# A mixture-of-experts decoder layer: experts of ranks 17 to 21 as blocks of 64 and 32 tokens on unsplit weights, a new order of blocks, twelve table tiles

## The chip, the cores and the metric

The kernel runs on one core of one Trainium2 chip. The metric is the device time of one execution in microseconds (us); lower is better. The input is one sequence of 2048 tokens with 1024 channels, in float32.

## The reference

One layer: a Conformer convolution mixer, then a mixture of 32 gated-MLP experts, each with a residual add, and a final RMSNorm. The change concerns the experts alone. In short:

```python
x = x + g1 * conformer_conv(h, ...)
h = rmsnorm(x, norm_ffn_g) * (1 + sc2) + sh2
# routing: the best of 4 groups, in it the best 2 of 8 experts, gate = p(group) * softmax(top 2)
for each expert e, for its tokens xb:
    hid = silu(xb @ w_gate[e]) * (xb @ w_up[e])      # 1024 -> 512
    y = hid @ w_down[e]                              # 512 -> 1024
    out[token] += gate * y
x = rmsnorm(x + g2 * out)
```

Each expert has 6.3 MB of weights (1024 x 512 twice and 512 x 1024, float32). The 4096 assignments (2048 tokens, two experts each) fall unevenly on the experts.

## The kernel before, in words

The first half of the run makes the convolution mixer and the routing, chunk by chunk; the change does not touch it. Its products on the expert side are a table per expert in DRAM (`tab_d`: token number, row to add to, gate), the normalized tokens (`x1n_d`) and the residual sum (`x2acc`), to which the experts' results are added by scatters.

*Ranks.* The experts are sorted by their number of tokens; rank p is a place in this sorting, and its expert number is read at run time (`number`, line 966, a load of `Ei` on SyncE, issued after the last weight load so far). `PROFILE` (line 48) says for each rank how many blocks of 128 tokens it has and how many tokens (32 or 64) one small block more takes. What a rank has beyond its profile goes through a loop at the end (`further_blocks`), which runs as often as there are such blocks.

*Two kinds of blocks.* A block of 128 tokens (b >= 0, "split") multiplies in three products: weights and tokens are each split into a high and a low part of type fp32r, and high x high, low x high and high x low are accumulated (`products`, lines 1068 to 1085). A small block (b < 0, "unsplit") multiplies the raw float32 weights once; with 64 tokens two column groups of the array work side by side, with 32 tokens four (m = 128 / tokens), each on its share of the contraction.

*Weights.* `load_expert` (line 990) loads an expert in six raw tiles of 1 MB (four of gate and up, two of down) from `RAWB` = 5 rotating buffers, all on SyncE's queue (line 998). If the rank has blocks of 128, ScalarE copies each raw half tile to its high part (line 1005) and VectorE subtracts (line 1006); the results fill `HLB` = 12 tiles, that is one expert. A raw tile is free when it is split and when the last unsplit matmul on it is done; a high or low tile when the last split block of its expert is done with it.

*Steps.* `ORDER` (line 64) lists all blocks as (rank, block), 50 of them; each becomes a `Step`. For step n the loop at the end of the kernel issues the gate and up matmuls, in their middle the transposes of step n-1's hidden values, then the activation, the gather of step n+2 (`ahead`), the load and token transposes of step n+1 (`start`), and the down matmuls and scatter of step n-1. A scheduler that orders each engine's instructions ahead of time may move them against this. `gather` (line 1020) loads the rank's tables when its first block comes (`load_table`, line 972): a tile `ft` for its blocks of 128 (line 979) and a tile `rt` for its small block (`small_rows`, line 724: 128 / tokens small loads and one VectorE instruction). Both have four buffers, and a table tile is in use until its block's scatter has landed. These loads stand in SyncE's queue among the weight loads. Gathers (line 1034) and scatters (line 1127) are issued by GpSimd.

*The end.* Rank 1 comes last. After its first block stand the overflow loop and the final normalization of all 2048 rows (`final_norm`), which reads what all other ranks have added; rank 1's own three blocks are normalized and written one by one (`norm`).

Of the kernel before, what the change touches and what calls it, by code (L numbers as in the profile page):

```python
# [13 lines left out]
I32 = mybir.dt.int32  # L14
# [7 lines left out]
P = 128  # L22
# [22 lines left out]

PROFILE = ([(3, 32), (3, 0), (2, 64), (2, 32), (2, 0), (1, 64), (1, 64)] + [(1, 32)] * 6 + [(1, 0)] * 9
           + [(0, 64)] * 8 + [(0, 32)] * 2)

EARLY = 2
EREST = PROFILE[0][1]
NEARLY = EARLY * 128 + EREST
# [4 lines left out]
LATE = 1  # L60
assert PROFILE[LATE][1] == 0


ORDER = [
# [5 lines left out]
]  # L70
RAWB, HLB = 5, 12
FIRSTL = 1
LASTU = 600

# [53 lines left out]
def moe_kernel(ctx, tc, x, xT, cols, ada, fing, w_in, w_out, b_r, wgu, wd, out):  # L128
    nc = tc.nc
# [15 lines left out]
    tabv = tab_d[:].rearrange("(e o b) c -> e o b c", o=P, b=NRB)  # L145
# [60 lines left out]
    def pool(name, bufs=1, stack=None, **kw):  # L206
        return (stack or p1).enter_context(tc.tile_pool(name=name, bufs=bufs, reuse_waits="tile", **kw))
# [484 lines left out]
    def first_rows():  # L692

        with urgent():
            pc = bank("acc", "pcs")
            nc.tensor.matmul(pc[:, :E], ones_bf[:], Cpre[:], start=True, stop=True)
            k = sm.tile([P, 2, E], F32, tag="fk", name="fk", bufs=1)
            V.tensor_tensor(k[:, 0], oh0[:], pc[:, :E], op=OP.mult)
            V.tensor_reduce(e0[:, 0:1], k[:, 0], axis=AX.X, op=OP.add)

            d = sm.tile([P, 1 + EARLY], F32, tag="fd", name="fd", bufs=1)
            for b in range((NEARLY + P - 1) // P):
                V.tensor_scalar(d[:, 1:2], pcol[:], e0[:, 0:1], float(b * P), op0=OP.add, op1=OP.add)
                V.tensor_scalar(d[:, 1:2], d[:, 1:2], float(NEARLY), None, op0=OP.is_lt)
                V.scalar_tensor_tensor(Cpre[:], oh0[:], d[:, 1:2], Cpre[:], op0=OP.mult, op1=OP.add)
            e = nc.sync.value_load(E0[0:1, 0:1], min_val=0, max_val=E - 1)
            ft = ep.tile([P, EARLY, 3], I32, name="fte")
            nc.sync.dma_start(ft[:], tabv[ds(e, 1), :, 0:EARLY, :].rearrange("e o b c -> (e o) b c"))
            rt = ep.tile([P, 3], I32, name="rte")
            small_rows(rt, e, EARLY, EREST)  # L710
            for b in range(-1, EARLY):
                m = P // EREST if b < 0 else 1
                t = rt if b < 0 else ft[:, b, :]
                xg = ep.tile([P, D // m], F32, name=f"xge{b + 1}")
                Q.indirect_dma_start(out=xg[:], out_offset=None, in_=x1n_d[:T0[-1], :].rearrange("t (m n) -> (t m) n", m=m),
                                     in_offset=bass.IndirectOffsetOnAxis(ap=t[:, 0:1].bitcast(U32), axis=0))
                early[b] = (t, xg)
            return e
# [2 lines left out]
    table_end = [None]  # L721
    sync = mybir.DependencyInfo(mybir.DependencyClass.Sync, mybir.DependencyReason.DATA)

    def small_rows(rt, e, b, rest):

        m = P // rest
        for g in range(m):
            nc.sync.dma_start(rt[g * rest:(g + 1) * rest, :], tabv[ds(e, 1), 0:rest, b, :].rearrange("e o c -> (e o) c"))
        V.tensor_scalar(rt[:, 0:2], rt[:, 0:2], float(m), pgrp[m][:], op0=OP.mult, op1=OP.add)

    wrv = col("w_r").rearrange("p (k n) -> p k n", k=KD)
# [69 lines left out]
    for s in range(NS + LAG_OUT):  # L801
        c, j = divmod(s, KD)
# [47 lines left out]
    for m in g2t:  # L850
        w, n = P // m, D // m
# [60 lines left out]
    nfull, cap, rest = (prof[:, q:q + 1] for q in range(3))  # L912
# [41 lines left out]
    xr = pool("xr", 1, p3)  # L954
# [8 lines left out]
    es, tix = {0: first}, {}  # L963
    loads, scattered = [], []

    def number(p):
        if p not in es:
            with tc.issue_after(loads[-1].ins):
                es[p] = nc.sync.value_load(Ei[0:1, p:p + 1], min_val=0, max_val=E - 1)
        return es[p]  # L970

    def load_table(p):

        nf, rest = PROFILE[p]
        ft = rt = None
        if nf:
            ft = xr.tile([P, 4, 3], I32, tag="ft", name="ft", bufs=4)
            if p:
                nc.sync.dma_start(ft[:, :nf, :], tabv[ds(number(p), 1), :, 0:nf, :].rearrange("e o b c -> (e o) b c"))
            else:  # L980
                for b in range(EARLY, nf):
                    for o, c, n in ((0, b, EREST), (P - EREST, b + 1, 0)):
                        nc.sync.dma_start(ft[o:o + (P - EREST if n else EREST), b, :],
                                          tabv[ds(number(p), 1), n:(P if n else EREST), c, :].rearrange("e o c -> (e o) c"))
        if p and rest:
            rt = xr.tile([P, 3], I32, tag="rt", name="rt", bufs=4)
            small_rows(rt, number(p), nf, rest)
        tix[p] = ft, rt

    def load_expert(p, tiles=range(6)):  # L990

# [2 lines left out]
        for n in tiles:  # L994
# [4 lines left out]
            raws.append((r,))  # L999
            if p is not None and PROFILE[p][0]:  # L1000
                h = hl[2 * n].tile([P, 2048], F32R, tag="hl", name="wh")
# [7 lines left out]
    class Step:  # L1009
# [10 lines left out]
        def gather(s):  # L1020
            if s.p == 0 and s.b in early:
                t, s.xg = early[s.b]
                s.entry(t)
                return
            if s.p not in tix:
                load_table(s.p)
            ft, rt = tix[s.p]
            t = ft[:, s.b, :] if s.split else rt
            s.entry(t)
            s.fetch()  # L1030

# [111 lines left out]

    steps = []
    for p, b in ORDER:
        steps.append(Step(p, b, 1 if b >= 0 else P // PROFILE[p][1]))
    ws = {}

    def start(s):
# [61 lines left out]
    for n in range(len(steps) + 1):  # L1211
        s = steps[n] if n < len(steps) else None
        t = steps[n - 1] if n > 0 else None
# [38 lines left out]
def host_layout(inputs):  # L1252
# [12 lines left out]
    prof = np.zeros((P, 3), np.float32)  # L1265
    for p, (n, r) in enumerate(PROFILE):
        prof[p] = (n, n * P + r, r)
# [40 lines left out]
```

## Time and profile before

| | us |
|---|---|
| median of 3 runs | 1640.28 |
| lowest and highest | 1636.06, 1649.84 |
| the profiled execution | 1638.36 |
| its span, first to last instruction | 1636.6 |

In the span TensorE is busy 1474.6 us (90%), VectorE 1116.2 (68%), ScalarE 977.9 (60%) and GpSimd 731.7 (45%). The expert stage begins near 828 us. An engine's busy time is the union of its instructions; an idle time is put down to what ended it. A matmul's end is modelled, so that neighbours overlap in the rows: the distance from one start to the next is what one costs. PE is TensorE, DVE VectorE, ACT ScalarE, POOL GpSimd, SPq SyncE's queue.

### The profile page before, as it was taken

The page shows a single profiled execution, that of the slowest core. Times are in us where ns is not written, and L with a number is a line of the kernel's source. Part 1 is how long each engine was busy: PE and PEld are TensorE (multiplying, and loading weights), DVE is VectorE, ACT ScalarE, POOL GpSimd, SP SyncE. Part 2 cuts the span into 40 slices and gives each one's busy share as a digit, 9 for nine tenths or more (in the row PEclk, how much of TensorE's full clock was granted, in tenths as well). Part 3 has the DMA queues.
Part 4 walks back from the last instruction along what each step waited for, and adds up shares of the span by engine and source line. Part 5 has one row for each costly group of instructions (what it writes and reads, how often), then busy time and mean ns, then how long its engine had stood idle before and what let it go on. Part 6 is the DMA issues. An engine that isn't in the chain of part 4 may idle for free. (4 is left out here: it accounts for less than half of the span.)

```text
span 1636.6 us, 24063 instructions
## 1 busy us (share of the span) xinstructions
PE 1474.6 (90%) x8269; PEld 1067.9 (65%) x8269; DVE 1116.2 (68%) x1777; ACT 977.9 (60%) x1602; POOL 731.7 (45%) x564
## 2 busy tenths in 40 slices
PE   6987997999889999987987899999999999898984
PEld 4765675677667777756854366556777767675663
DVE  2564988688988899885462257254588778786465
ACT  5576768766876788445440255234487668675553
POOL 0268699768778787854231122121122212122222
PEclk9988999899999999998999999999999999999997
DMA  8696796776766558594548999989899889887987
GB/s 323 234 367 240 245 297 211 254 257 241 254 242 214 184 193 289 189 309 147 220 140 230 370 343 355 344 292 376 310 383 346 306 276 383 284 339 213 367 309 268
DMA packets 123646, 455.98 MB, mean 279 GB/s; under 512 B 25594, under 2 KB 29058, under 8 KB 98946
## 3 DMA queue, kind: packets, MB, share of 16 engines
q1 hardware_dynamic: 93842, 362.48, 61.7%
q0 software_dynamic: 14224, 40.43, 9.8%
q10 hardware_dynamic: 15456, 51.51, 7.9%
q8 instruction: 66, 1.08, 0.3%
q14 instruction: 58, 0.48, 0.1%
HBM read 374.24 MB, written 80.13 MB: 278 GB/s over the span
## 5 line engine op out<-in xcount | busy, mean ns | idle before, releaser
L467 POOL TENSOR_TENSOR acc<-acc,prod 128x512 f32<-128x512 f32 x321 | 426.9, 1330 | 59.2 <-ACT prod L461 38.0
L473 DVE SCALAR_TENSOR_TENSOR acc<-u,colt,acc 128x512 f32<-128x512 f32 x497 | 371.3, 751 | 49.3 <-PE acc L444 39.5
L1006 DVE TENSOR_TENSOR wl<-wraw,wh 128x1024 fp32r<-128x1024 f32 x260 | 304.9, 1218 | 53.0 <-ACT wh L1005 51.6
L461 ACT ACTIVATE prod<-u,colt 128x512 f32<-128x512 f32 x385 | 268.8, 720 | 91.7 <-POOL acc L467 74.7
L1005 ACT ACTIVATE wh<-wraw 128x1024 fp32r<-128x1024 f32 x264 | 265.0, 1059 | 87.8 <-DMA wraw<-in_wgu 43.0
L1082 PE MATMUL pg<-wh,xh 128*128 128x512 f32 x464 | 150.5, 399 | 13.6 <-ACT wh L1005 7.5
L1082 PE MATMUL pg<-wl,xh 128*128 128x512 f32 x464 | 149.0, 396 | 0.9 <-DVE wl L1006 0.7
L1082 PE MATMUL pg<-wh,xl 128*128 128x512 f32 x464 | 149.0, 396 | 0.0
L1084 PE MATMUL pg<-wraw,xh 128*32 128x256 f32 (+1 forms) x992 | 121.9, 470 | 5.9 <-DMA wraw<-in_wgu 3.4
L1034 POOL DMA_INDIRECT xg<-x1n_d,ft x27 | 33.7, 1250 | 203.4 <-DMA rt<-tab_d 75.3
L1051 ACT ACTIVATE psx<-psx,modc,A 128x128 f32<-128x128 f32 x232 | 90.3, 441 | 52.0 <-PE psx L1046 37.1
L1127 POOL DMA_INDIRECT x2acc<-ys,ft x24 | 57.5, 2398 | 142.6 <-DVE ys L1124 119.0
L371 PE MATMUL pg<-hh,wh 128*128 128x512 f32 x256 | 106.6, 416 | 14.0 <-DMA wh<-wi_d 9.8
L1082 PEld LDWEIGHTS pg<-wh,xh 128*128 128x128 f32 x464 | 87.2, 190 | 38.0 <-ACT wh L1005 10.6
L371 PE MATMUL pa<-hh,wh 128*128 128x512 f32 x256 | 103.2, 403 | 7.1 <-DVE u L408 6.6
L1100 ACT ACTIVATE sg<-pg 128x256 f32<-128x256 f32 (+1 forms) x79 | 26.3, 370 | 135.5 <-PE pg L1082 66.9
L373 PE MATMUL pg<-hh,wl 128*128 128x512 f32 x256 | 104.7, 409 | 1.5 <-DMA wl<-wi_d 1.5
L1127 POOL DMA_INDIRECT x2acc<-ys,rt x20 | 33.5, 1673 | 160.5 <-DVE ys L1124 111.9
L372 PE MATMUL pg<-hl,wh 128*128 128x512 f32 x256 | 105.1, 411 | 0.0
L371 PE MATMUL po<-zz,wh 128*128 128x512 f32 (+1 forms) x256 | 96.9, 384 | 7.8 <-ACT zz L332 7.8
L372 PE MATMUL pa<-hl,wh 128*128 128x512 f32 x256 | 102.1, 399 | 0.0
L373 PE MATMUL pa<-hh,wl 128*128 128x512 f32 x256 | 102.1, 399 | 0.0
(276 smaller groups left out, 2937.9 us busy)
## 6 DMA issues: line engine op xcount, KB each, us to landing
wraw<-in_wgu SPq DMA_DIRECT2D x128, 1024.0 KB, 8.8
wraw<-in_wd SPq DMA_DIRECT2D x64, 1024.0 KB, 8.5
adar<-in_ada SPq DMA_DIRECT2D x48, 512.0 KB, 4.0
wh<-wi_d SPq DMA_DIRECT2D x42, 512.0 KB, 3.5
wl<-wi_d SPq DMA_DIRECT2D x42, 512.0 KB, 5.1
wraw<-in_w_in SPq DMA_DIRECT2D x22, 512.0 KB, 7.2
wh<-wo_d SPq DMA_DIRECT2D x20, 512.0 KB, 3.8
wl<-wo_d SPq DMA_DIRECT2D x20, 512.0 KB
```

Source lines behind the costliest of these rows:

```text
L371: nc.tensor.matmul(po[:, :n], wh, xh[:, :n], start=(k == 0), stop=False)
L372: nc.tensor.matmul(po[:, :n], wh, xl[:, :n], start=False, stop=False)
L373: nc.tensor.matmul(po[:, :n], wl, xh[:, :n], start=False, stop=(k == KD - 1))
L461: S.activation(pr[:, :n], u[:, k:k + n], AF.Copy, scale=wdw[:, k:k + 1])
L467: Q.tensor_tensor(acc2[:, :n], acc2[:, :n], pr[:, :n], op=OP.add)
L473: V.scalar_tensor_tensor(acc, u[:, k:k + n], wdw[:, k:k + 1], acc, op0=OP.mult, op1=OP.add)
L1005: S.activation(h[:, o], r[:, o], AF.Copy)
L1006: (Q if len(ws) == 1 and n % 3 == 2 else V).tensor_tensor(l[:, o], r[:, o], h[:, o].bitcast(F32), op=OP.subtract)
L1051: S.activation(ps[:, q, :], ps[:, q, :], AF.Identity, bias=modc[:, 24 + k:25 + k], scale=A2[:, k:k + 1])
L1082: nc.tensor.matmul(outs[o][:], st[x], mv, start=a, stop=z)
L1084: nc.tensor.matmul(outs[0][o * w:(o + 1) * w, :n], st[x], mv, start=a, stop=z, tile_position=(0, o * w))
L1127: Q.indirect_dma_start(out=x2acc[:].rearrange("t (m n) -> (t m) n", m=s.m), out_offset=bass.IndirectOffsetOnAxis(ap=s.si, axis=0), in_=ys[ ...
```

## The change

Ranks 17 to 21 get profile (0, 96) in place of (1, 0): no block of 128, and small blocks of 64 and 32 tokens (`SMALL`), so that their weights are not split. A rank's small blocks are numbered -1 and -2; each has an `rt` tile of its own, the second one read from row 64 of the table on. `ft` and `rt` get twelve buffers in place of four. `ORDER` is a new one, of 55 blocks.

```diff
--- before.py
+++ after.py
@@ -45,8 +45,10 @@
 
 
 
-PROFILE = ([(3, 32), (3, 0), (2, 64), (2, 32), (2, 0), (1, 64), (1, 64)] + [(1, 32)] * 6 + [(1, 0)] * 9
-           + [(0, 64)] * 8 + [(0, 32)] * 2)
+
+PROFILE = ([(3, 32), (3, 0), (2, 64), (2, 32), (2, 0), (1, 64), (1, 64)] + [(1, 32)] * 6 + [(1, 0)] * 4
+           + [(0, 96)] * 5 + [(0, 64)] * 8 + [(0, 32)] * 2)
+SMALL = {0: [], 32: [32], 64: [64], 96: [64, 32]}
 
 
 
@@ -62,13 +64,13 @@
 
 
 ORDER = [
-    (0, -1), (0, 0), (0, 1), (22, -1), (25, -1), (23, -1), (0, 2), (20, 0), (28, -1), (21, 0), (2, -1), (2, 0),
-    (27, -1), (26, -1), (2, 1), (3, -1), (3, 0), (29, -1), (24, -1), (3, 1), (4, 0), (30, -1), (4, 1), (9, -1),
-    (9, 0), (19, 0), (14, 0), (17, 0), (5, -1), (5, 0), (8, -1), (8, 0), (7, -1), (7, 0), (11, -1), (11, 0),
-    (16, 0), (15, 0), (13, 0), (18, 0), (6, -1), (6, 0), (12, -1), (12, 0), (10, -1), (10, 0), (31, -1), (1, 0),
-    (1, 1), (1, 2),
+    (0, -1), (0, 0), (0, 1), (31, -1), (23, -1), (0, 2), (9, -1), (9, 0), (25, -1), (16, 0), (2, -1), (28, -1),
+    (2, 0), (30, -1), (24, -1), (2, 1), (4, 0), (26, -1), (4, 1), (15, 0), (12, -1), (19, -1), (19, -2),
+    (12, 0), (5, -1), (21, -1), (21, -2), (5, 0), (7, -1), (17, -1), (17, -2), (7, 0), (13, 0), (27, -1),
+    (6, -1), (6, 0), (10, -1), (20, -1), (20, -2), (10, 0), (11, -1), (11, 0), (29, -1), (8, -1), (8, 0),
+    (3, -1), (22, -1), (18, -1), (18, -2), (3, 0), (3, 1), (14, 0), (1, 0), (1, 1), (1, 2)
 ]
-RAWB, HLB = 5, 12
+RAWB, HLB, TB = 5, 12, 12
 FIRSTL = 1
 LASTU = 600
 
@@ -721,11 +723,12 @@
     table_end = [None]
     sync = mybir.DependencyInfo(mybir.DependencyClass.Sync, mybir.DependencyReason.DATA)
 
-    def small_rows(rt, e, b, rest):
+    def small_rows(rt, e, b, rest, o=0):
 
         m = P // rest
         for g in range(m):
-            nc.sync.dma_start(rt[g * rest:(g + 1) * rest, :], tabv[ds(e, 1), 0:rest, b, :].rearrange("e o c -> (e o) c"))
+            nc.sync.dma_start(rt[g * rest:(g + 1) * rest, :],
+                              tabv[ds(e, 1), o:o + rest, b, :].rearrange("e o c -> (e o) c"))
         V.tensor_scalar(rt[:, 0:2], rt[:, 0:2], float(m), pgrp[m][:], op0=OP.mult, op1=OP.add)
 
     wrv = col("w_r").rearrange("p (k n) -> p k n", k=KD)
@@ -972,9 +975,9 @@
     def load_table(p):
 
         nf, rest = PROFILE[p]
-        ft = rt = None
+        ft = None
         if nf:
-            ft = xr.tile([P, 4, 3], I32, tag="ft", name="ft", bufs=4)
+            ft = xr.tile([P, 4, 3], I32, tag="ft", name="ft", bufs=TB)
             if p:
                 nc.sync.dma_start(ft[:, :nf, :], tabv[ds(number(p), 1), :, 0:nf, :].rearrange("e o b c -> (e o) b c"))
             else:
@@ -982,10 +985,11 @@
                     for o, c, n in ((0, b, EREST), (P - EREST, b + 1, 0)):
                         nc.sync.dma_start(ft[o:o + (P - EREST if n else EREST), b, :],
                                           tabv[ds(number(p), 1), n:(P if n else EREST), c, :].rearrange("e o c -> (e o) c"))
-        if p and rest:
-            rt = xr.tile([P, 3], I32, tag="rt", name="rt", bufs=4)
-            small_rows(rt, number(p), nf, rest)
-        tix[p] = ft, rt
+        rts = {}
+        for i, n in enumerate(SMALL[rest] if p else []):
+            rts[-1 - i] = xr.tile([P, 3], I32, tag="rt", name="rt", bufs=TB)
+            small_rows(rts[-1 - i], number(p), nf, n, sum(SMALL[rest][:i]))
+        tix[p] = ft, rts
 
     def load_expert(p, tiles=range(6)):
 
@@ -1024,8 +1028,8 @@
                 return
             if s.p not in tix:
                 load_table(s.p)
-            ft, rt = tix[s.p]
-            t = ft[:, s.b, :] if s.split else rt
+            ft, rts = tix[s.p]
+            t = ft[:, s.b, :] if s.split else rts[s.b]
             s.entry(t)
             s.fetch()
 
@@ -1143,7 +1147,7 @@
 
     steps = []
     for p, b in ORDER:
-        steps.append(Step(p, b, 1 if b >= 0 else P // PROFILE[p][1]))
+        steps.append(Step(p, b, 1 if b >= 0 else P // SMALL[PROFILE[p][1]][-1 - b]))
     ws = {}
 
     def start(s):
```

## Rows read from the trace of the kernel before

**Rows 1.** Stretches (us from start): length, then each engine's busy time, clock, DMA share.

```profile
858.00:926.00 68.00, 51.42 (x248) 23.67 (x246) 11.67 (x22) 6.30 (x17) 11.97 (x9) 0.95 0.90 291
926.00:1100.00 174.00, 165.31 (x829) 103.89 (x831) 94.12 (x121) 77.92 (x129) 36.53 (x24) 1.00 0.93 336
1100.00:1400.00 300.00, 295.31 (x1715) 213.75 (x1712) 211.35 (x253) 199.64 (x324) 63.85 (x40) 1.00 0.95 341
1400.00:1500.00 100.00, 86.75 (x425) 62.16 (x424) 76.01 (x86) 65.15 (x94) 24.40 (x11) 0.91 0.82 278
1500.00:1570.00 70.00, 62.98 (x449) 44.88 (x447) 44.23 (x55) 40.04 (x68) 15.60 (x10) 0.99 0.87 308
```

**Rows 2.** Waits of TensorE, 858 to 1616 us: total, times, longest.

```profile
PE psx L1046 <- DMA xg<-x1n_d,rt: 17.5, 4, 8.0
PE pg L1082 <- ACT wh L1005: 7.5, 3, 4.8
PE pd L1082 <- ACT hidh L1109: 6.0, 8, 1.4
```

**Rows 3.** Waits of SyncE's queue, 820 us to the end.

```profile
SPq L998 <- DVE wl L1006: 164.5, 65, 7.6
SPq L998 <- PE pd L1084: 157.0, 31, 15.7
SPq L998 <- PE pg L1084: 105.8, 40, 16.1
...
SPq L979 <- DMA x2acc<-ys,ft: 26.1, 5, 9.4
```

**Rows 4.** Timeline of TensorE, a split block: start, length, instruction, count.

```profile
950.51 0.62 PE L1082 MATMUL pg<-wh,xh 128*128 128x512 f32 x2
...
960.94 0.61 PE L1082 MATMUL pg<-wl,xh 128*128 128x512 f32 x2
...
967.28 1.04 PE L1046 MATMUL psx<-ident,xg 128*128 128x128 f32 x8
```

**Rows 5.** Timeline of TensorE, blocks of 64 and 32 tokens.

```profile
1020.86 3.65 PE L1084 MATMUL pd<-wraw,hidh 128*64 128x512 f32 x16
...
1027.35 7.09 PE L1084 MATMUL pg<-wraw,xh 128*64 128x512 f32 x32 [0.40 <-DVE xh L1062]
...
1181.97 3.66 PE L1084 MATMUL pg<-wraw,xh 128*32 128x256 f32 x64
...
1549.37 1.93 PE L1084 MATMUL pd<-wraw,hidh 128*32 128x256 f32 x32 [0.59 <-ACT psx L1051]
```

**Rows 6.** Groups by line, 830 us on: count, busy us, mean ns, idle before.

```profile
L1006 DVE TENSOR_TENSOR wl<-wraw,wh 128x1024 fp32r<-128x1024 f32 x252 | 295.5, 1218 | 50.9 <-ACT wh L1005 49.5 <-PE psx L1046 0.5
L1005 ACT ACTIVATE wh<-wraw 128x1024 fp32r<-128x1024 f32 x254 | 255.1, 1059 | 86.5 <-DMA wraw<-in_wgu 43.0 <-PE pg L1082 14.2 <-PE pd L1082 12.8
```

**Rows 7.** Timeline of SyncE, a table load.

```profile
1416.24 0.34 SPq L979 DMA_DIRECT2D ft<-tab_d  x1
```

**Rows 8.** Timeline of TensorE, two waits (idle before, and what ended it).

```profile
1426.28 0.79 PE L1082 MATMUL pg<-wh,xh 128*128 128x512 f32 x1 [4.76 <-ACT wh L1005]
...
1485.54 0.69 PE L1046 MATMUL psx<-ident,xg 128*128 128x128 f32 x2 [6.50 <-DMA xg<-x1n_d,rt]
```

**Rows 9.** DMA queues, 820 us to the end: packets, MB, share.

```profile
q1 hardware_dynamic: 35904, 204.56, 65.4%
q0 software_dynamic: 12992, 39.21, 19.1%
```

**Rows 10.** Timeline of TensorE and SyncE, the expert stage's start.

```profile
827.67 5.37 PE L1084 MATMUL pg<-wraw,xh 128*32 128x256 f32 x64 [2.06 <-DVE xh L1062]
...
849.79 0.35 SPq L998 DMA_DIRECT2D wraw<-in_wgu  x1
```

**Rows 11.** Raw weight tiles, 840 to 1570 us.

```profile
DMA to landing us min/median/max: 5.1/8.7/13.3
```

**Rows 12.** Timeline of SyncE, four loads behind a hold.

```profile
1050.86 15.25 SPq L998 DMA_DIRECT2D wraw<-in_wgu  x4
```

## The prediction, made blind

> **What bounds the kernel now.** I read the page's slices first: in the expert stage, the second half, TensorE and the DMA engines are both near nine tenths. Cut into stretches [rows 1], TensorE idles 16.6 us of the first 68, then 8.7 of 174, 4.7 of 300, 13.3 of 100 and 7.0 of the last 70 before the final normalization gets going; the DMA share is 0.82 to 0.95. VectorE and ScalarE are 70% and 67% busy in the 300 us where TensorE idles least. So the stage is a race of two nearly full resources, and a change to it is worth what it takes from TensorE's work or from its idle time, some 50 us in all.
>
> Who ended that idle time is in TensorE's waits [rows 2]: gathered tokens 17.5 us, split weights that were not ready 7.5, split hidden values 6.0. SyncE's queue, which issues every weight load, says why [rows 3]: it waited 164.5 us until VectorE had split a raw tile, 157.0 and 105.8 until TensorE had let go of one, and 26.1 us, in five waits, until a scatter had let go of one of the four table tiles.
>
> **The change, part by part.** The routing worked out from the reference gives ranks 17 to 21 94, 83, 79, 78 and 68 tokens, all above 64 and none above 96: each does get a 64 and a 32 block.
>
> *TensorE's work: -2.5 us.* The 48 gate and up matmuls of a split block run in 24 pairs, the first at 950.51 and the last at 960.94, so 0.45 us a pair and 10.9 us in all; its 24 down matmuls at that pace take 5.5, and its 12 transposes, at 1.04 us for eight, 1.6: 18.0 us [rows 4]. A 64 block takes 7.09 + 3.65 and half the transposes, 11.5; a 32 block 3.66 + 1.93 and a quarter, 6.0 [rows 5]. Five times (17.5 - 18.0) is -2.5 us: the unsplit blocks win next to nothing on TensorE.
>
> A rule would speak against them. In rows 5 the four unsplit groups cost what they last, and TensorE's waits name no switch of array shape. The Trainium skill (TensorEngine Tiling (Array Packing), Key Properties) says that switching the tiling mode drains the engine. If a drain cost a pair's overlap (0.62 us busy against 0.45 from one to the next), some 40 more switches would add 7 us; by the rows they add nothing, and the sum goes by the rows.
>
> *VectorE and ScalarE, and the table tiles: -17 us.* Twelve half tiles per expert are no longer split: 12 x 1.218 = 14.6 us of VectorE and 12 x 1.059 = 12.7 of ScalarE, 73 and 64 us over five experts [rows 6]. As a mean neither is the bound, so this counts where split experts of one block follow each other, and there are four in a row just before 1450. There SyncE stood at the next table until 1416.24, one of the five waits for a scatter [rows 7]; the loads behind it left late, and TensorE waited 4.76 us for split weights at 1421 and 6.50 at 1479 for tokens, whose table had come late in the same lagging queue [rows 8]. Twelve table tiles take that wait away, and the new order has no four such experts in a row: the stretch's 13.3 us of idle time go. The clock granted in it was 0.91, a mean of its two levels (1.00 is 2.4 GHz, the other 1.2), against 1.00 in the two stretches before, where TensorE hardly stood [rows 1]; (1 - 0.91) x 86.75 us busy is at most 8 us more, and I take half, 4. Bounds: 0 (the lag comes back elsewhere) and -21. What is late next is the weight stream itself, two terms on.
>
> *DMA traffic.* Weights stay 32 times 6 tiles. 204.56 MB took 65.4% of 816.6 us, so a 1.05 MB tile takes 2.74 us and an expert 16.4. Gathers and scatters took 19.1%, 156 us, for 39.21 MB in 12992 packets [rows 9]: a 128 block (1.05 MB, 256 packets) costs 4.2 us by bytes or 3.1 by packets, a 64 block 2.1 or 3.1, a 32 block 1.0 or 3.1. A changed expert costs 1.1 us less by bytes, 3.1 more by packets; both ends go into the next term. The five more gathers and scatters that GpSimd issues and 25 more small table loads on SyncE stand in queues that mostly wait for raw tiles or results, and I price them at nothing beyond that; without that cover they would cost what they take to issue, half a microsecond to two each, 10 to 25 us.
>
> *The order: +10 us.* Loads past the first expert begin at 849.8, when the sort is known; TensorE starts at 827.7 [rows 10]. I walked both orders: an expert is wanted when TensorE's work before it is done, and ready at 849.8 + 16.4 us for it and for each one before it + the block traffic of all earlier steps + 5.1 us to land, the shortest seen [rows 11]. The first, for example: wanted at 827.7 + 6.0 + 2 x 18.0 = 869.7, ready at 849.8 + 16.4 + 9.4 + 5.1 = 880.7, so TensorE stands 11 us. By bytes the old order waits 30.6 us, all before 1050 (11, 7 and 7 for the first three, 6 later). The new one waits 43.4: 11 and 11 for ranks 31 and 23, 7 for 28, 5 for 24, 3 for 19, 6 for 18. By packets it is 32.1 against 68.0. The old order really idled 25.3 us up to 1100 [rows 1], eight tenths of its walk, since the walk wants an expert whole where a block can start on its first tile. Eight tenths of 12.8 is +10. Bounds: 0, if the blocks can be interleaved around each gap, and +36.
>
> *The tail: +2 us.* The last expert before rank 1 is now a split one (14) where it was a 32 block (31). The final normalization may read only when the last scatter before it has landed; the down matmuls behind that take 5.5 us where they took 1.9, and half of the difference I let show. Bounds 0 and 8.
>
> *Sum.* -2.5 - 17.3 + 10 + 2 = -7.8 us. On the profiled execution (1638.36 us, its span 1636.6) that is 1630.6; the median shown is 1.9 us higher, within the spread of the three runs. I forecast **1631 us**.
>
> **Rivals.** *Held raw tiles (slower).* The change keeps raw weights of five experts through two blocks each, on five raw tiles; their down tiles are let go only when the second block is through too. Each such hold grows by the 32 block's 3.66 and 1.93 us, 5.6 us [rows 5]. Where loading is not 5.6 us ahead of need, TensorE pays it; in the walk by bytes it is 5 to 17 us ahead behind most of the five and not ahead at all at 19 and 18. All five in full are +28: 1659 us. For it: 263 us of SyncE's waits are already for raw tiles that TensorE holds [rows 3], and in before one expert's four issues stretched over 15.25 us behind such a hold [rows 12]. Against it: the DMA share was still 0.95 in the middle.
>
> *The relief reaches every stall (faster).* If early tables and freer VectorE and ScalarE remove all idle time from 926 to 1570 (33.7 us) and the 4 us of clock, and the order costs nothing: 1640 - 33.7 - 4 - 2.5 + 2 = 1602 us. For it: tokens, split weights and split hidden values ended 31 of TensorE's 53 us. Against it: one token wait of 8.0 us lies where the queue waits for raw tiles of the first experts, and no term of the change touches it.
>
> *The change does not do what it says.* If one of the five had over 96 tokens on the chip, the overflow loop would load its weights again and run a whole unsplit block behind the branch: 16.4 + 5.1 us and four times a 32 block's 6.0, near 1677. The largest count leaves two tokens of room.
>
> **How the numbers follow.** Forecast 0.45, its own range 1617 to 1646; held tiles 0.28; full relief 0.25; overflow 0.02. One per cent, about what a measurement of this kernel can tell from no change, is 1624 and 1657. Faster: the relief and a fifth of the forecast's range, 0.34. Slower: two thirds of the held tiles, around their price, and the overflow, 0.22. Same: 0.44. The range, 1604 to 1660, leaves out the best of the relief and the worst of the holds.
>
> **What would show it.** Right: no idle of TensorE over 4 us between 1000 and 1500; no wait of SyncE for a scatter at the table load; VectorE some 75 and ScalarE some 65 us less busy; TensorE's busy time within 10 us of before; the first 100 us as poor as now. Held tiles: SyncE's waits for TensorE's unsplit matmuls well above 263 us, DMA share in the middle below 0.90, TensorE idle for weights around ranks 19 and 18. Relief: TensorE above 97% from 930 us to the branch. The forecast is wrong if the start costs over 10 us more, or if the lag of the single split experts returns behind the five.

## The result, and the profile after

The changed kernel takes 1694.69 us in the median (1688.56 to 1706.37, four runs) against 1643.57 for the kernel before (1636.06 to 1649.84): a ratio of 1.035, 95% interval [1.031, 1.039]. The forecast was 1631 us, with a range up to 1660. It is slower: the medians are 51 us apart, and the ratio times 1640, the measure used below, makes it 58.

The profiled execution took 1691.11 us with a span of 1689.3. First its stretches, as in [rows 1], from the window view; the last row is the whole expert stage, from its first matmul to its last, and the fence behind it has the same row of the kernel before.

```profile
858.00:926.00 68.00, 53.62 (x323) 34.02 (x323) 17.36 (x36) 11.04 (x23) 12.31 (x10) 0.90 0.84 268
926.00:1100.00 174.00, 161.36 (x849) 96.24 (x846) 86.47 (x111) 72.36 (x121) 35.46 (x23) 0.96 0.96 343
1100.00:1200.00 100.00, 94.44 (x564) 58.65 (x566) 58.95 (x77) 49.96 (x81) 22.43 (x16) 0.99 0.91 316
1200.00:1300.00 100.00, 93.81 (x627) 50.76 (x623) 43.33 (x59) 37.61 (x64) 19.49 (x13) 1.00 0.86 295
1300.00:1400.00 100.00, 88.48 (x501) 50.76 (x500) 55.01 (x71) 40.89 (x62) 19.38 (x13) 0.95 0.85 307
1400.00:1500.00 100.00, 89.89 (x607) 57.01 (x606) 58.06 (x76) 49.20 (x81) 22.59 (x15) 0.95 0.83 292
...
833.20:1667.90 834.70, 753.38 (x4368) 468.40 (x4368) 417.84 (x611) 349.11 (x592) 179.84 (x130) 0.96 0.85 297
```

```profile
827.70:1616.10 788.40, 733.92 (x4023) 504.37 (x4023) 483.05 (x656) 422.51 (x696) 176.64 (x120) 0.98 0.89 316
```

The stage is 46.3 us longer. TensorE's idle time (length less busy) rose from 54.5 to 81.3 us, its busy time by 19.5. The second is mostly the clock: 1 - 0.96 of 834.7 us is 33 us of full speed lost, 1 - 0.98 of 788.4 is 16, so 17 to 18 more (with two digits of the clock, give or take 4 on each). The clock of the whole span has three digits, 0.960 of 1636.6 us and 0.951 of 1689.3, and gives 17 us more as well. The other 6 us lie ahead of the stage (833.2 against 827.7) and behind it. The middle, 1100 to 1400, had 4.7 us of idle time at a DMA share of 0.95; it now has 23.3 at 0.85 to 0.91, with the same weight traffic (204.57 MB on the weights' queue against 204.56). So the weight stream stands still more often; the experiments show what that does to the time.

SyncE's waits are to be read against [rows 3], TensorE's against [rows 2] (total, times, longest):

```profile
SPq L1002 <- DVE wl L1010: 173.8, 42, 22.4
SPq L1002 <- PE pg L1088: 157.8, 54, 16.7
SPq L1002 <- PE pd L1088: 149.6, 40, 16.6
```

```profile
PE psx L1050 <- DMA xg<-x1n_d,rt: 19.8, 4, 11.7
PE psh L1111 <- DVE sg L1105: 11.4, 7, 4.3
PE pg L1086 <- issue: 10.4, 1, 10.4
PE pg L1088 <- DVE xh L1066: 10.3, 5, 4.9
PE pd L1088 <- ACT hidh L1113: 9.5, 5, 3.3
PE pg L1088 <- DMA wraw<-in_wgu: 8.6, 8, 4.4
```

The wait for a scatter at the table load is gone, as forecast. SyncE's waits until TensorE lets go of a raw tile rose from 263 to 307 us: that and the lower DMA share in the middle are marks that the prediction gave for its rival of held tiles; the third, TensorE idle for weights, is small (8.6 us in eight waits). The work itself changed as planned: in the stage VectorE is 65 us less busy and ScalarE 73. Of the splitting ([rows 6]) 194 half tiles are left, 66.6 us of VectorE less:

```profile
L1010 DVE TENSOR_TENSOR wl<-wraw,wh 128x1024 fp32r<-128x1024 f32 x194 | 228.9, 1219 | 68.4 <-ACT wh L1009 65.8 <-PE pg L1086 2.0
```

What stands before TensorE's longest wait is in the timelines of SyncE, GpSimd and TensorE:

```profile
870.38 7.87 SPq L1002 DMA_DIRECT2D wraw<-in_wd  x2
879.05 1.24 SPq L730 DMA_DIRECT2D rt<-tab_d  x2
...
885.58 1.58 POOL L1131 DMA_INDIRECT x2acc<-ys,fte  x1 [12.88 <-DMA x2acc<-ys,rte]
888.83 1.00 POOL L1038 DMA_INDIRECT xg<-x1n_d,ft  x1 [1.66 <-DMA ft<-tab_d]
890.13 0.98 POOL L1038 DMA_INDIRECT xg<-x1n_d,rt  x1 [0.30 <-issue]
...
899.19 1.12 PE L1050 MATMUL psx<-ident,xg 128*128 128x128 f32 x4 [11.71 <-DMA xg<-x1n_d,rt]
```

Two weight loads wait for raw tiles that TensorE still reads. The tables of the next blocks stand behind them in the same queue, the gathers need the tables, and TensorE stood idle from 887.5 for 11.7 us. Here, though, the queue is the smaller part: GpSimd was held until 885.6 by an earlier scatter that had not landed, and of the tables it then waited 1.7 us. This start is poor in the kernel before, too (8.0 us). Further on, the experiments show waits that the queue alone makes.

### The profile page after: what moved, and what is told of

The parts are those of the page before. It is cut to its first block, busy times and chain, and to the rows that moved or that the text cites. A ratio compares the mean times of both kernels' runs of the same rounds, so it can differ in the third digit from the quotient of the medians.

```text
span 1689.3 us, 24717 instructions
## 1 busy us (share of the span) xinstructions
PE 1495.5 (89%) x8614; PEld 1031.8 (61%) x8614; DVE 1052.0 (62%) x1732; ACT 904.0 (54%) x1497; POOL 735.0 (44%) x574
## 5 line engine op out<-in xcount | busy, mean ns | idle before, releaser
L1010 DVE TENSOR_TENSOR wl<-wraw,wh 128x1024 fp32r<-128x1024 f32 x200 | 237.0, 1224 | 70.5 <-ACT wh L1009 66.4
L1009 ACT ACTIVATE wh<-wraw 128x1024 fp32r<-128x1024 f32 x204 | 204.8, 1056 | 122.7 <-DMA wraw<-in_wgu 53.5
L1088 PE MATMUL pg<-wraw,xh 128*32 128x256 f32 (+1 forms) x1472 | 192.4, 484 | 21.9 <-DVE xh L1066 13.4
L1131 POOL DMA_INDIRECT x2acc<-ys,rt x30 | 51.0, 1701 | 221.8 <-DVE ys L1128 88.7
L1088 PEld LDWEIGHTS pg<-wraw,xh 128*32 128x32 f32 (+1 forms) x1472 | 64.8, 126 | 129.8 <-issue 82.9
L1086 PE MATMUL pg<-wh,xh 128*128 128x512 f32 x384 | 125.9, 401 | 10.4 <-issue 10.4
L1086 PE MATMUL pg<-wh,xl 128*128 128x512 f32 x384 | 123.7, 396 | 0.2 <-DVE xl L1070 0.2
L1086 PE MATMUL pg<-wl,xh 128*128 128x512 f32 x384 | 122.2, 392 | 0.0
L1088 PE MATMUL pd<-wraw,hidh 128*32 128x256 f32 (+1 forms) x736 | 97.7, 478 | 11.5 <-ACT hidh L1113 9.5
L373 PE MATMUL po<-zz,wh 128*128 128x512 f32 (+1 forms) x256 | 96.9, 384 | 8.8 <-ACT zz L334 7.7
L374 PE MATMUL po<-zz,wh 128*128 128x512 f32 (+1 forms) x256 | 98.0, 384 | 1.6 <-DVE zz L335 1.6
```

The lines of the kernel that those rows point to most:

```text
L373: nc.tensor.matmul(po[:, :n], wh, xh[:, :n], start=(k == 0), stop=False)
L374: nc.tensor.matmul(po[:, :n], wh, xl[:, :n], start=False, stop=False)
L1009: S.activation(h[:, o], r[:, o], AF.Copy)
L1010: (Q if len(ws) == 1 and n % 3 == 2 else V).tensor_tensor(l[:, o], r[:, o], h[:, o].bitcast(F32), op=OP.subtract)
L1086: nc.tensor.matmul(outs[o][:], st[x], mv, start=a, stop=z)
L1088: nc.tensor.matmul(outs[0][o * w:(o + 1) * w, :n], st[x], mv, start=a, stop=z, tile_position=(0, o * w))
```

## The experiments

One theory, **held tiles** (raw tiles that unsplit blocks hold stop the weight stream, the rival of the prediction), is set against its rivals, in turn the tail, the table tiles, the blocks' own work, the order of the traffic, and chains of short blocks. All ratios are to the kernel before, run beside them; their intervals reach 3 to 8 us to either side.

**Each part alone.** Four kernels. The first is the kernel before with `TB = 12`.

> The kernel before with one edit: twelve buffers for the table tiles in place of four (old order, ranks 17 to 21 split). Held raw tiles as the cause: this edit is harmless or good, 1622 to 1645 us; the 26 us that SyncE waited for scatters at a table load are gone and with them some of the 11 us that TensorE stood at 1421 and 1479. More table tiles as the cause (they let the small loads run ahead and block the weight loads behind them): above 1660 us.

Measured: 1636.87 us, ratio 0.9991 [0.9968, 1.0015]. Twelve table tiles do nothing for the time by themselves. SyncE's waits for a scatter at a table load fell from 26.1 to 0.2 us, and the stretch from 1400 to 1500 got better (idle time 8.3 us in place of 13.3, clock 0.97 in place of 0.91); the whole did not.

The second has the changed kernel's blocks in the old order:

```diff
-    ... (20, 0), (28, -1), (21, 0), ... (19, 0), (14, 0), (17, 0), ... (18, 0), ...
+    ... (20, -1), (20, -2), (28, -1), (21, -1), (21, -2), ... (19, -1), (19, -2), (14, 0), (17, -1), (17, -2), ...
```

> The changed kernel with the old order, in which each of the five experts' single block is replaced in its place by its two unsplit blocks. Held raw tiles as the cause: slower than before by 25 us or more, above 1668 us, with the DMA share in the middle below 0.90 around ranks 17 to 21. The new order as the cause: within 12 us of before, 1632 to 1655 us.

Measured: 1691.59, 1.0332 [1.0287, 1.0377]. The third has the new order, but ranks 17 to 21 split as before, each just behind the split block that its pair stood in front of (18 behind the second of rank 3's two).

> The new order with twelve table tiles, but ranks 17 to 21 as one split block each; since the split tiles hold one expert only, each of the five stands just behind the split block that it stood in front of. Held raw tiles as the cause: most of the loss is gone, 1645 to 1668 us, the rest being the start and the split expert 14 ahead of the overflow loop. The order as the cause: 1680 us or more.

Measured: 1685.76, 1.0291 [1.0251, 1.0331]. The fourth is the changed kernel with (14, 0) and (29, -1) exchanged, so that a small block stands last before rank 1.

> The changed kernel with two places of its order exchanged: the unsplit rank 29 stands ahead of rank 1, and the split rank 14 where 29 stood. If the split expert ahead of the overflow loop costs what the traces suggest (TensorE stands 10.4 us at the loop in place of 5.0, and its 6 us of down matmuls and transposes come behind rank 1's first block), 8 to 16 us faster than the changed kernel, 1679 to 1687 us. If the tail is not at fault: within 5 us of 1695.

Measured: 1695.55, 1.0354 [1.0313, 1.0395]: TensorE's wait at the loop fell from 10.4 to 6.0 us, and the time stayed. So the unsplit pairs alone cost 54 us, the new order alone 48, and both together 58: they do not add up, which speaks for a resource that both exhaust.

**Who holds what.** In four kernels chosen unsplit blocks multiply by a constant tile in place of the raw weights. Loads, gathers, matmuls and scatters stay; only nobody holds those raw tiles once they have landed.

```diff
                     mv = ws[y][:, (k % 2) * D + o * c:(k % 2) * D + (o + 1) * c]
+                    if s.p in range(17, 22):
+                        mv = g2t[1][:, o * c:(o + 1) * c]
```

> The unsplit blocks alone in the old order (a_oldorder, 1691.6 us, some 53 over before), and in it the ten blocks of ranks 17 to 21 take their weights from a constant tile of SBUF (the g2 row) in place of the five experts' raw tiles. The loads, the gathers, the matmuls, the transposes and the scatters stay, only nobody holds these 30 raw tiles after they land. Leaves out: the products of ranks 17 to 21 with their own weights. Theory held tiles (the 53 us are the weight stream standing still while five raw tiles are held for two blocks): the 53 us go, and a little more, since these experts' tiles now also skip the splitting: 1620 to 1645 us. Rival, the work itself (more TensorE instructions, chains of small blocks, gathers and scatters of two blocks in place of one): the time stays within 15 us of 1691.

Measured: 1665.53, 1.0147 [1.0099, 1.0195].

> As a_old_c, but only the five blocks of 32 tokens take the constant tile; the blocks of 64 still read the raw tiles. Leaves out: the products of the 32-token blocks of ranks 17 to 21 with their own weights. Theory held tiles: a raw tile now comes free after the first of two blocks, as with any expert of one unsplit block. If the cost goes with the time for which a tile is held (17.5 us of blocks, of which 6.0 are the second's), 53 x 6.0 / 17.5 = 18 us go: about 1673; if only the second block's hold hurts (the first is covered as for the ten other unsplit experts), most of the 53 goes: 1640 to 1655. Rival, the work itself: within 15 us of 1691.

Measured: 1659.26, 1.0107 [1.0070, 1.0144]. Both lie outside every range that was expected. Without the second blocks' hold two thirds of the 54 us are gone: held tiles, not the work, which is still all there. That the freer of the two (a_old_c) is not the faster shows that weights are not all of it. In the trace of a_old_c SyncE's queue stood 19.6 us at two weight loads, at which it waited, by the profile, for an unsplit matmul (16.7 us the longest), and the tables of rank 2 came after that:

```profile
950.17 19.55 SPq L1002 DMA_DIRECT2D wraw<-in_wd  x2
971.11 8.06 SPq L1002 DMA_DIRECT2D wraw<-in_wgu  x4
981.80 3.07 SPq L1002 DMA_DIRECT2D wraw<-in_wd  x2
985.65 0.33 SPq L982 DMA_DIRECT2D ft<-tab_d  x1
986.18 1.14 SPq L730 DMA_DIRECT2D rt<-tab_d  x2
...
996.33 0.98 POOL L1038 DMA_INDIRECT xg<-x1n_d,rt  x1 [0.31 <-issue]
...
1005.63 1.08 PE L1050 MATMUL psx<-ident,xg 128*128 128x128 f32 x4 [11.70 <-DMA xg<-x1n_d,rt]
```

TensorE waited 11.7 us for rows, not for weights. The same with every unsplit block on the constant tile, in the kernel before and in the new order:

> The kernel before, all of whose unsplit blocks (ranks 22 to 31 and the small blocks of split experts) take their weights from the constant tile, so that no raw tile is ever held by TensorE; raw tiles are held only until they are split. Leaves out: the products of those blocks with their own weights. Theory held tiles: SyncE's 263 us of waits for unsplit matmuls go and part of them comes back as waits for the splitting or for landings; a walk of the load order with five raw tiles, 3.7 us a tile and the traced order of blocks puts the gain at 35 us: 1595 to 1620. Rival (the waits for raw tiles are covered, the end is set by the transfers' own rate or by TensorE): within 10 us of 1638.

Measured: 1641.75, 1.0008 [0.9988, 1.0028]: in the kernel before the holds cost nothing of the whole time, against my 35 us. It also shows that the constant tile by itself makes nothing faster (a 64 block's gate and up matmul takes 608 ns in the mean with it, 599 with raw weights).

> The new order with all of ranks 17 to 21 split (b_neworder, 1685.8 us, some 48 over before), and in it no unsplit block holds a raw tile, as in b_allc. Leaves out the same products. To be read against b_allc. Theory held tiles: the new order costs its 48 us because its unsplit blocks stand so that raw tiles are held at bad places: within 10 us of b_allc. Rival 1, the split experts' high and low tiles (one expert's set, held until its last split block; in the new order SyncE waited 231 us for the splitting against 165): 20 to 48 us over b_allc; the same walk puts it at 24. Rival 2, the order of gathers and scatters: also over b_allc, but with SyncE's waits for the splitting not above b_allc's.

Measured: 1649.27, 1.0029 [1.0000, 1.0059]: in the new order they are nearly all of its 48 us. The rivals named there, the high and low tiles and the order of gathers and scatters, wanted 20 us or more over b_allc; it is 3 by the ratios.

**Tables out of the blocked queue.** If a blocked weight load does harm through the tables behind it, loading the tables earlier must help, with no weight any earlier. Nothing is left out in these four kernels (the old-order control has twelve table tiles):

```diff
             if n + 2 != new:
                 ahead(n + 2)
+            if n + 1 >= new:
+                with tc.high_priority(offset=MOE_URGENT):
+                    for t_ in steps[n + 3:n + 3 + 4]:
+                        if t_.p not in tix:
+                            load_table(t_.p)
```

> The unsplit blocks alone in the old order (a_oldorder, 1691.6 us), with nothing left out, but each expert's table of rows is loaded four steps earlier, so that in SyncE's queue it stands ahead of the weight tiles of the experts between. Theory queue: a weight load that waits for a raw tile which an unsplit block still holds stands in SyncE's queue in front of the table loads of the next blocks (in a_oldorder one pair of loads of down weights held the queue for 17.3 us, the eight table loads followed at 965.0, the gather at 973.6, and TensorE stood idle for 8.8 us until 980.5); tables, gathers and TensorE are late by that, and the clock falls after such an idle. Then TensorE's 41 us of waits for gathered rows fall below 15, its idle time from 81 to about 55 us and the loss by the clock from 33 to about 16: 1645 to 1665 us. Rival, held tiles alone (it is the weights that come late, whatever the tables do): within 10 us of 1691, with the waits for rows replaced by waits for weights and their splitting.

Measured: 1664.55, 1.0172 [1.0128, 1.0215]. The timeline of the old order without this edit, around the end of rank 20's pair, and two windows of it:

```profile
946.95 17.28 SPq L1002 DMA_DIRECT2D wraw<-in_wd  x2
965.04 5.52 SPq L730 DMA_DIRECT2D rt<-tab_d  x8
...
973.57 1.01 POOL L1038 DMA_INDIRECT xg<-x1n_d,rt  x1 [8.67 <-DVE rt L732]
...
980.52 1.09 PE L1050 MATMUL psx<-ident,xg 128*128 128x128 f32 x4 [8.82 <-DMA xg<-x1n_d,rt]
```

```profile
940.00:970.00 30.00, 28.07 (x173) 13.94 (x173) 6.18 (x12) 2.30 (x6) 3.21 (x2) 1.00 0.49 147
970.00:1000.00 30.00, 19.15 (x101) 6.70 (x97) 6.06 (x13) 1.05 (x3) 6.20 (x5) 0.83 0.93 324
```

While the queue stands, the DMA share is 0.49; then TensorE stands 8.8 us, and the granted clock of the next window is 0.83. With the edit, at the same place:

```profile
958.50 1.14 SPq L730 DMA_DIRECT2D rt<-tab_d  x2
959.88 6.74 SPq L1002 DMA_DIRECT2D wraw<-in_wgu  x4
...
969.79 3.40 PE L1088 MATMUL pg<-wraw,xh 128*64 128x512 f32 x8 [2.71 <-DMA wraw<-in_wgu]
973.78 1.94 PE L1088 MATMUL pg<-wraw,xh 128*64 128x512 f32 x8 [0.58 <-DMA wraw<-in_wgu]
977.45 1.94 PE L1088 MATMUL pg<-wraw,xh 128*64 128x512 f32 x8 [1.74 <-DMA wraw<-in_wgu]
```

TensorE starts the next block's products at 969.8, but now waits for its weights, piece by piece: the second way in which a held tile costs. Over the stage the waits for rows fell from 41.1 to 5.6 us, and TensorE's idle time from 81.0 to 53.2, as expected; the clock came back half way, to 0.97.

> The changed kernel (1694.7 us) with the tables loaded four steps earlier, nothing left out. Theory queue: its 20 us of waits for gathered rows fall below 8, and part of the waits behind late rows (VectorE's xh 13, sg 12) with them: 1655 to 1680 us. Rival, held tiles alone: within 10 us of 1692.

Measured: 1676.03, 1.0229 [1.0185, 1.0274].

> The new order with ranks 17 to 21 split (b_neworder, 1685.8 us) with the tables loaded four steps earlier, nothing left out. Theory queue: 27 us of waits for rows go, of them 10.8 at 890 us and 10.4 at 1481 us, and some 10 us of clock: 1645 to 1670 us. Rival, held tiles alone: within 10 us of 1686.

Measured: 1660.89, 1.0131 [1.0083, 1.0180].

> The kernel before with twelve table tiles (b_tb12, 1636.9 us) with the tables loaded four steps earlier, nothing left out. Theory queue: its 17 us of waits for rows go and it gains as much, 1615 to 1630 us; the gain is smaller than that of the two kernels above, since less is held. Rival, held tiles alone: within 8 us of 1637.

Measured: 1640.31, 1.0015 [0.9988, 1.0041]. By the ratios late tables are 26 us in the old order, 20 in the changed kernel and 26 in the new order (with intervals this wide, the three do not differ), and nothing in the kernel before, where I had expected 7 to 22. From 905 us on, TensorE waits for rows nowhere in these four traces; at the start it still does (6.8 us in a_tab), where the queue issues the first tables at the same time as before the edit (879.1).

**Both remedies together, and a finer ring.** First, tables early and the five 32 blocks on the constant tile:

> Both remedies in the old order with unsplit blocks: tables four steps earlier (a_old_tab, 1664.6 us) and the five blocks of 32 tokens on the constant tile, so that they hold no raw tile (a_old_c2, 1659.3). Leaves out: the products of those five blocks with their own weights. Theory held tiles, by two ways (late tables and late weights): what is left over b_tab (1640.3) goes: 1635 to 1650 us. Rival, the short blocks as such (chains of transposes and activations, more gathers): the two remedies act on the same 27 us, and it stays at 1655 to 1665.

Measured: 1644.76, 1.0036 [1.0016, 1.0056]. In the old order 48 of the unsplit pairs' 54 us are accounted for. How they are shared out depends on what is taken first: early tables give 26 and the freed second blocks then 22, or the freed second blocks give 37 and early tables then 12. So the two overlap: much of the tables' lateness comes from the second blocks' hold, and the last 12 us of it from other holds.

> The same two remedies in the changed kernel (a_tab, 1676.0 us). Leaves out the same products. Theory held tiles, second blocks: 1645 to 1658. Rival, the new order: its own rest (b_new_tab stands 21 us over b_tab) stays: 1660 to 1676, since the small blocks of split experts still hold theirs.

Measured: 1672.88, 1.0203 [1.0170, 1.0237]. The rival holds here: the new order keeps its own rest, and the second blocks' hold is worth 4 us by the ratios in it, no more than the intervals.

> The changed kernel with the tables earlier (a_tab, 1676.0 us) and ten raw tiles of half the size in place of five, each loaded, split and released by itself; nothing left out, SBUF the same. Theory held tiles: each half comes free earlier, by half the time that a tile is read or split (some 1.2 us in VectorE's splitting, 0.9 to 1.8 us of TensorE), and the ring holds what is needed more closely: 5 to 20 us faster, 1656 to 1671. Rival (loads of 512 KB with rows of 4 KB are less efficient, twice as many issues in SyncE's queue): no gain or slower, 1676 to 1700.

Measured: 1687.69, 1.0293 [1.0260, 1.0326].

> The same half tiles in the kernel before with early tables (b_tab, 1640.3 us), nothing left out. In this kernel taking the unsplit blocks' hold away brought nothing (b_allc), so theory held tiles expects little: 1628 to 1642. Rival (smaller loads cost): 1645 to 1665.

Measured: 1650.86, 1.0083 [1.0051, 1.0114]. The edit loads `[P, 1024]` into ten tiles where it loaded `[P, 2048]` into five. What was meant to help costs 10 to 12 us in both. In the rows of the DMA queues from 820 to 1690 us, of b_tab with whole tiles and then of b_half_tab, the same bytes take 63.9% of the engines' time in place of 61.7, so 19 us more:

```profile
q1 hardware_dynamic: 35904, 204.56, 61.7%
```

```profile
q1 hardware_dynamic: 62832, 204.57, 63.9%
```

The Trainium skill (DMA: Bandwidth & Descriptors, Bandwidth) advises loads of 1 MiB or more, measured there on loads that GpSimd issued; these two runs, with SyncE's loads of 512 KB against 1024, agree. Half the load is also half the row (4 KB against 8); the two were not told apart.

**What the new order's rest is.** The last two:

> The changed kernel, tables four steps earlier, and every unsplit block on the constant tile, so that none holds a raw tile (as b_allc, 1641.8, and b_new_allc, 1649.3). Leaves out: the products of all unsplit blocks with their own weights. Theory held tiles (of the other unsplit blocks too): 1640 to 1655. Rival, chains of short blocks (three unsplit blocks in a row; TensorE waits for VectorE's and ScalarE's steps between gate/up, transposes and down, which no weight tile touches; in a_tab_c2 psh waited 21.7 us, against 5.8 in before): 1662 to 1676.

Measured: 1628.43, 0.9937 [0.9915, 0.9960]. Below both ranges, and not the chains of short blocks: with no raw tile held by an unsplit block and the tables early, the changed kernel's blocks and order are 10 us faster than before.

> The new order with ranks 17 to 21 split and early tables (b_new_tab, 1660.9 us), and only the small unsplit blocks of split experts on the constant tile; the ten unsplit experts 22 to 31 still hold theirs. Leaves out: the products of those small blocks with their own weights. Theory held tiles by the small blocks: 1638 to 1650. Rival, held by the experts 22 to 31, or no hold at all: 1654 to 1665.

Measured: 1636.30, 0.9998 [0.9975, 1.0020]. The new order's rest is the hold of the split experts' own small blocks: from 1.0131 to 0.9998, 22 us. SyncE's waits for TensorE's unsplit matmuls, with them and without:

```profile
SPq L1002 <- PE pg L1088: 138.6, 42, 18.8
SPq L1002 <- PE pd L1088: 92.6, 35, 11.7
```

```profile
SPq L1002 <- PE pg L1090: 75.6, 25, 10.8
SPq L1002 <- PE pd L1090: 37.4, 13, 7.7
```

| us over before, by the ratios, at 1640 | as built | tables early | and freed |
|---|---|---|---|
| pairs, old order | 54 | 28 | 6 (32 blocks) |
| new order, all split | 48 | 21 | 0 (small blocks of split experts) |
| both | 58 | 38 | 33 (32 blocks), -10 (all unsplit blocks) |

No kernel that computes everything beat the one before.

## Why the prediction was wrong

The view of the whole was right: a race of two nearly full resources, in which five raw tiles are scarce. The rival that was named, held raw tiles, is what happened, given 0.28 and too small a price. (Two thirds of 0.28 and the overflow's 0.02 make 0.21 for slower, where 0.22 stands.) By its steps:

- *TensorE's work, -2.5 us.* Not the cause. Its busy time rose by 19.5 us, but in a_tab_allc, with the same blocks and the clock of before (0.98), it is 737.4 us against 733.9: some 4 us of work in place of -2.5, the rest goes with the clock. The mean of a 64 block's gate and up matmuls rose from 599 to 621 ns; in a_tab_allc it is 598, so the extra switches of array shape do not make the rise.
- *VectorE, ScalarE and table tiles, -17.3 us: the first step that failed.* The cited wait for a scatter did go, and 12 table tiles alone brought nothing (b_tb12), although they took 5 us of idle time and most of the clock's loss out of the stretch. The 6.5 us for tokens stayed there (6.3): they were not the table tiles' doing, and early tables, which did remove them, brought the kernel before nothing either (b_tab). One stretch's stall was priced as if the whole run got shorter by it; it did not, and why not is open (see below on the start of the stage). In the changed kernel TensorE idled 10.1 us from 1400 to 1500, and new waits came elsewhere. The working had that end of its range ("the lag comes back elsewhere") and did not choose it.
- *The order, +10 us: mis-sized, 48 alone, and by another mechanism.* The walk asked when weights can be there and took raw tiles as always free. Its stalls at the start did not come: from 858 to 1100 TensorE idled 27.0 us where it had idled 25.3, and waited 1.1 us for raw weights. In the kernel before that was 4.1 us, against 11.9 for tokens, so the eight tenths scaled the walk by idle time of other causes. What the order changed is which tiles are held when. With the small blocks' hold gone and the tables early nothing of it is left (b_new_tab_sc), so the supply that the walk priced is not what costs. Its other end, +36 by packets, was nearer by luck.
- *The small loads in SyncE's queue, "at nothing beyond that".* Not priced: 20 to 26 us in the three slower kernels, the only part that a run which computes everything took back. I took the queue's waits as cover for the table loads; they are the reverse, since what stands behind a waiting load in SyncE's queue waited too (17.28 us in a_oldorder), and after it the gathers and TensorE.
- *Held raw tiles, 5.6 us for each of five experts, 28 in all.* Alone it measured 54. The price counted the direct way only, late weights. With the tables early a_old_tab is 28 us over before; that this is the rival's number is partly luck, since the 28 hold the clock, too, and 6 of them stay when the second blocks hold nothing (a_old_tab_c2). The tables behind the queue and the lower clock around each stop were not counted.
- *The tail, +2 us.* No effect within the interval: a_tail took 4.4 us off the wait at the loop and the time did not change.
- *Full relief and overflow.* Neither came; the weights' queue moved no expert twice (204.57 MB against 204.56). That freeing VectorE and ScalarE can be worth something shows only in a_tab_allc, and there with everything else freed too.

What stays open: why the small blocks' holds cost some 22 us in the new order and nothing in the old one (b_allc), with as many such blocks in both. The runs show that they do, not by which sequence of blocks. That the two parts do not add up is consistent with one exhausted ring, but it was not tested beyond these runs. The 6 us outside the stage were not traced either: the first expert matmul lay between 826.9 and 838.7 us in kernels whose first half has the same instructions. This bears on the small differences: in the traces of b_tb12, b_allc and a_tab_allc the stage is 8, 10 and 14 us shorter than before, and it begins 10, 8 and 11 us later. With one trace of each, no run shows whether the late start belongs to the kernel or to that execution. "Nothing", for the holds and for the table tiles of the kernel before, is said of the whole time; in the stage it may hide some 10 us.

## What to carry over

When a buffer is scarce, price a change by how long it keeps each one, and for every load that must wait for it look up what stands behind that load in the same queue. Small loads that start a chain (tables, then gathers, then TensorE) belong ahead of the large ones that may wait; that was worth 20 to 26 us where the queue stood long, and nothing in the kernel before. What a stall lasts in one stretch is not yet what its removal is worth: twelve table tiles took 5 us of idle time out of one, and the time stayed. And a stall of TensorE cost more than itself here, since the clock was lower around it.

## What was not expected

Of the hardware: the clock took 17 to 18 us beside the 27 of added stalls, two thirds as much again. Over the stage the granted clock was 0.98 in the kernel before and 0.96 in the changed one, a mean of the two levels (1.00 is 2.4 GHz, the other 1.2); in a_oldorder it was 1.00 in the 30 us before TensorE's stop of 8.8 us and 0.83 in the 30 us that held it. And the Trainium skill (DMA: Bandwidth & Descriptors, Issuing engines are not separate DMA queues) says that spreading issues over engines saves only the issuing time, usually small. What it says of transfers does not cover a load that waits for a buffer: here one queue's order was worth 26 us (a_old_tab against a_oldorder), with not one transfer fewer. Another issuing engine for the tables was not tried.
